# Relative bias read straight from one small table of reversed distances, without per-row copies in DRAM, and the compressed blocks' bias from the same table

## The chip, the cores and the metric

The kernel runs on one core of a Trainium2 chip. The metric is device time in microseconds (us) of one execution; 1440.13 us is the median of 3 runs of the kernel before (1440.06 to 1442.18). The engines are TensorE (PE, matmuls; PEld are its weight loads), VectorE (DVE), ScalarE (ACT), GpSimd (POOL) and SyncE (SP, which here only issues DMAs).

## The reference, cut to what matters

Four layers over 256 tokens of 1024 features: layers 0 and 3 are differential attention, layer 1 is a three-branch sparse attention (compressed blocks, selected blocks, window), layer 2 is attention with a forget gate. Each layer then has a feed-forward part and a gated embedding. Layers 0, 1 and 3 add to every score a bias that depends only on the head and on a bucket of the distance between query and key:

```python
bias = rel_bias[t5_bucket(dist)]            # dist = query position - key position, 32 buckets x 16 heads
s = einsum('bqhcd,bkhcd->bhcqk', qb, k) * scale + bias
pr = masked_softmax(s, dist >= 0)           # layers 0 and 3: 8 pairs of heads, pr[:,:,0] - lam * pr[:,:,1]
...
d_c = t[:, None] - cmp_end[None, :]         # layer 1: distance to the end of block n, cmp_end = 16 n + 31
s_c = einsum('bqgrd,bngd->bgrqn', qc, kc) * scale + rel[t5_bucket(d_c)]
```

## The kernel before

All matmuls of weights run in three passes: an activation on ACT (line 148, `wh`) and a subtraction on DVE (line 149, `wl`) split each 512 KB unit of weights, `raw`, into a high and a low part, and PE multiplies both (lines 170 to 172). `raw` has 5 buffers and is filled by SP; `wh` and `wl` have 8 each. A tile scheduler fixes the order of each engine's instructions when the kernel is built; at run time each engine takes its own list strictly in order. All DMAs of the bias are issued from ACT's list (`QS` is a string of "a" only).

Layer 0 (`diff`) goes like this. `v_proj` projects the values of both token tiles of 128; when tile 0 is done, `between` calls `bias_rows` (line 369): a matmul of a one-hot table of buckets with `rel_bias` gives 16 rows of 512 values, negated bias or a huge number where the key lies ahead of the query, and these go to DRAM as `row`. Then four copies from DRAM to DRAM (line 383) write each head's row 128 times at a pitch of 384 values: `skew`, 4 tiles of 768 KB. `bias_load` (line 409) reads the copies with a step that is one value short of the pitch, so that partition i gets the row shifted by i: `nb`, 128 partitions x 4 heads x 256 keys, two buffers, 12 loads in all, 4 in each of layers 0, 1 and 3. Then `heads` runs the steps of `SEQ`: `K0`, `Q0` and so on split weights, `k0` and `q0` project keys and queries of four heads (`lin_b`, evacuated by ACT at line 436), two digits start an item (four heads of one token tile): scores on PE (line 538), `soft` (line 428 on DVE adds the bias and takes the minimum of the negated scores, line 432 on ACT takes the exponential), transposes (line 506) and products with the values (line 513). The step `b` calls `bias_blocks` (line 395), which loads the one-hot table in the other direction and runs 15 matmuls (line 402) for the 15 compressed blocks, and keeps the result in DRAM as `cmpb`; layer 1 (`nsa`) loads it into the tile `own` (line 755). The output projection follows, then the feed-forward part.

Of the kernel before, what the change touches and what calls it, by code (L numbers as in the profile page):

```python
# [18 lines left out]
P = 128  # L19
# [36 lines left out]
SD = "q0.k0.00.q1.k1.01.10.11.q2.k2.20.21.p.q3.k3.30.p.b.31"  # L56
SEQ = {0: 'K0.Q0.Q1.k0.q0.K1.00.k1.q1.K2.01.Q2.k2.10.q2.20.p.11.21.q3.K3.k3.p.p.p.b.30.31.O.O.O', 2: 'k1.q2.Q0.q1.q0.10.k0.p.11.k3.q3.b.00.01.k2.p.20.p.30.21.p.31', 3: 'K0.Q0.Q1.k0.q0.K1.q1.00.k1.K2.01.Q2.k2.10.q2.20.p.11.21.q3.p.k3.p.p.b.30.31.O.O.O'}
SKEW = 384
# [10 lines left out]
def bucket_table():  # L69
    t = np.zeros((33, 2, 512), np.float32)  # L70
    v = np.arange(512)
    for way, dist in ((0, 255 - v), (1, v - 256)):
        t[rel_bucket(dist), way, v] = -1.0
        t[32, way, v] = (dist < 0).astype(np.float32)
    return t


def shape_consts():
    i = np.arange(P)
    c = np.zeros((P, 2 * P + 1), np.float32)  # L80
    c[:, 0:P] = i[:, None] <= i[None, :]
    c[:, P : 2 * P] = np.where(i[None, :] > i[:, None], BIG, 0.0)
    c[:, 2 * P] = i >= 31
    return c


class Trunk:
# [69 lines left out]
    def unit(self, src, k0, nk, c0, nc):  # L157
        """Rows of chunks k0..k0+nk and columns c0..c0+nc, split: [128, nk, nc]."""
# [3 lines left out]
    def panel(self, src, c0, nc, nk, early=()):  # L162
        """All of 1024 rows in units of nk chunks; [k] gives chunk k's parts [128, nc]."""
# [15 lines left out]
    def later(self, n, key, fn):  # L179
        """Runs fn, which fills a part of key's tiles, after n more products, to issue behind them."""  # L180
# [6 lines left out]
    def flush(self, keys):  # L187
        """Before keys' tiles are read: runs what still has to fill them."""
# [33 lines left out]
    def transpose_split(self, src, hi, lo, t, scale=None, n=KD, c0=0, lag=()):  # L222
        """src [128 tok, n*128] -> hi/lo[:, c0 + c, t*128:(t+1)*128]."""
# [23 lines left out]
    def rms_halves(self, halves):  # L247
        """1 / rms of [half 0, half 1]; each half's square is taken when it is ready."""
# [14 lines left out]
    def prenorm(self, t, g, hT, lag=()):  # L263
        """After the last change of x[t]; takes its halves one after the other."""
# [30 lines left out]
    def startnorm_(self, t, g, hT):  # L295
        """prenorm of the input as it arrives; the second step transposes."""
# [24 lines left out]
    def lin_a(self, src, c0, aT, done, mix, pj=False, cuts=None, early=()):  # L321
        """y[t] = a @ src[:, c0 : c0 + 1024]; token tile 0 runs before tile 1."""
# [12 lines left out]
    def mul_a(self, y, a, w, first, mix):  # L335
        """y += a @ w over a list of chunks. The last ones end the sum, its first half mix chunks ahead of its second."""
# [7 lines left out]
    def lin_b(self, src, c0, hT, w=None):  # L344
        """[256 columns from c0, transposed] = (h @ src)^T in one bank: [128, 2, 256]."""
# [12 lines left out]
    def consts(self):  # L358
# [7 lines left out]
        self.skew = None  # L366
        self.cmp_bias = None

    def bias_rows(self):
        """The bias of every distance, one row per head, then once per query row at a pitch of SKEW."""  # L370
        nc = self.nc
        oh, tab = self.bias_operands(0)
# [4 lines left out]
        row = self.dr.tile([NH, 512], F32, tag="row", name="row")  # L377
        self.dq[QS[0]].dma_start(row, rs)
        self.skew = []
        for u in range(4):  # L380
            sk = self.dr.tile([4, P, SKEW], F32, tag=f"skew{u}", name=f"skew{u}")
            src = bass.AP(tensor=row.tensor, offset=row.offset + 4 * u * 512, ap=[[512, 4], [0, P], [1, SKEW]])
            self.dq[QS[1]].dma_start(sk, src)  # L383
            self.skew.append(sk)

    def bias_operands(self, way):
        nc, a = self.nc, self.a
        oh = self.m2([33, 512])
        nc.sync.dma_start(oh, a["buckets"][:, way, :])
        tab = self.small([33, NH])  # L390
        nc.gpsimd.memset(tab, BIG)
        nc.sync.dma_start(tab[0:32, :], a["rel_bias"])
        return oh, tab
# [762 lines left out]
```

## Time and profile before

| what | value |
|---|---|
| median of 3 runs, lowest, highest | 1440.13, 1440.06, 1442.18 us |
| span of the profiled execution, first to last instruction | 1449.6 us |
| PE busy | 1411.0 us (97% of the span), 8814 instructions |
| DVE, ACT, POOL busy | 855.8, 755.1, 71.9 us |
| mean granted PE clock | 0.979 of full |
| read from HBM, written | 247.61 MB, 4.43 MB |

The span is the profiled execution's own time; no separate time was taken of it, and it is 9.5 us above the median of the runs. PE is busy nearly everywhere, so time can come only from stretches in which PE waits, runs at a lower clock or does work that goes away. Stages are best told apart by stretches of time: layer 0's values end at 37.7 us and its output projection at 168.1 us; the same stage of layer 3 lies at 1139.2 to 1238.7 us.

### The profile page before, as it was taken

The page shows a single profiled execution, that of the slowest core. Times are in us where ns is not written, and L with a number is a line of the kernel's source. Part 1 is how long each engine was busy: PE and PEld are TensorE (multiplying, and loading weights), DVE is VectorE, ACT ScalarE, POOL GpSimd, SP SyncE. Part 2 cuts the span into 40 slices and gives each one's busy share as a digit, 9 for nine tenths or more (in the row PEclk, how much of TensorE's full clock was granted, in tenths as well). Part 3 has the DMA queues.
Part 4 walks back from the last instruction along what each step waited for, and adds up shares of the span by engine and source line. Part 5 has one row for each costly group of instructions (what it writes and reads, how often), then busy time and mean ns, then how long its engine had stood idle before and what let it go on. Part 6 is the DMA issues. An engine that isn't in the chain of part 4 may idle for free.

```text
span 1449.6 us, 22594 instructions
## 1 busy us (share of the span) xinstructions
PE 1411.0 (97%) x8814; PEld 1225.6 (85%) x8814; DVE 855.8 (59%) x1495; ACT 755.1 (52%) x1239; POOL 71.9 (5%) x116
## 2 busy tenths in 40 slices
PE   8589999999999999999999999999999999999998
PEld 6588898998888678998987987998988987999987
DVE  5265765556637656655566555755557577855545
ACT  4255555444625565554446555645446656644443
POOL 1000200000100001000001000000001001100000
PEclk9888999999999899999999999999999999999999
DMA  8564465655575204655645742765646643655642
GB/s 298 177 209 136 136 217 173 202 190 180 164 216 177 77 30 146 225 185 173 202 160 157 257 138 87 233 191 173 203 138 213 221 141 109 213 194 175 203 146 73
DMA packets 155042, 251.41 MB, mean 173 GB/s; under 512 B 10294, under 2 KB 119782, under 8 KB 154936
## 3 DMA queue, kind: packets, MB, share of 16 engines
q1 hardware_dynamic: 144312, 236.44, 50.1%
q10 hardware_dynamic: 10624, 13.53, 3.0%
q8 instruction: 69, 1.13, 0.3%
q14 instruction: 37, 0.30, 0.1%
HBM read 247.61 MB, written 4.43 MB: 174 GB/s over the span
## 4 chain that ended last, share of the span: by engine, by line
PE 68%; issue 21%; DMA 3%; POOL 3%; DVE 2%; ACTq 2%; ACT 2%; DVEq 0%; SPq 0%; POOLq 0%
PE pj L170 11%; PE pj L171 10%; PE pj L172 10%; PE acc L170 9%; PE acc L171 9%; PE acc L172 9%; PE wk L234 2%; PE acc L538 2%; DMA nb<-skew 2%; ACTq L383 2%; PE acc L907 1%; POOL small L213 1%; PE pj L698 1%; PE wk L513 1%; PE wk L658 1%
## 5 line engine op out<-in xcount | busy, mean ns | idle before, releaser
L149 DVE TENSOR_TENSOR wl<-raw,wh 128x1024 fp32r<-128x1024 f32 x421 | 509.9, 1221 | 356.4 <-ACT wh L148 342.6
L148 ACT ACTIVATE wh<-raw 128x1024 fp32r<-128x1024 f32 x421 | 441.9, 1057 | 364.4 <-PE acc L171 149.8
L170 PE MATMUL pj<-big,wh 128*128 128x256 f32 x1248 | 357.2, 286 | 11.8 <-ACT wh L148 11.8
L171 PE MATMUL pj<-big,wl 128*128 128x256 f32 x1248 | 356.2, 285 | 1.1 <-DVE wl L149 1.1
L172 PE MATMUL pj<-big,wh 128*128 128x256 f32 x1248 | 355.5, 285 | 0.0
L170 PEld LDWEIGHTS pj<-big,wh 128*128 128x128 f32 x1248 | 241.1, 193 | 16.2 <-ACT wh L148 12.3
L171 PEld LDWEIGHTS pj<-big,wl 128*128 128x128 f32 x1248 | 241.1, 193 | 5.0 <-DVE wl L149 2.2
L172 PEld LDWEIGHTS pj<-big,wh 128*128 128x128 f32 x1248 | 241.1, 193 | 0.3
L170 PE MATMUL acc<-wh,s 128*128 128x512 f32 x512 | 200.3, 391 | 0.0
L171 PE MATMUL acc<-wh,s 128*128 128x512 f32 x512 | 199.6, 390 | 0.0
L172 PE MATMUL acc<-wl,s 128*128 128x512 f32 x512 | 199.3, 389 | 0.0
L170 PE MATMUL acc<-wh,big 128*128 128x512 f32 (+2 forms) x344 | 132.0, 384 | 0.0
L171 PE MATMUL acc<-wh,big 128*128 128x512 f32 (+2 forms) x344 | 131.1, 381 | 0.0
L172 PE MATMUL acc<-wl,big 128*128 128x512 f32 (+2 forms) x344 | 130.3, 380 | 0.0
L172 PEld LDWEIGHTS acc<-wl,s 128*128 128x128 f32 x512 | 96.1, 188 | 20.3
L170 PEld LDWEIGHTS acc<-wh,s 128*128 128x128 f32 x512 | 96.2, 188 | 18.9
L171 PEld LDWEIGHTS acc<-wh,s 128*128 128x128 f32 x512 | 96.3, 188 | 18.8
L170 PE MATMUL pj<-wh,big 128*128 128x256 f32 (+1 forms) x320 | 100.3, 315 | 0.3 <-ACT big L241 0.2
L171 PE MATMUL pj<-wh,big 128*128 128x256 f32 (+1 forms) x320 | 98.7, 309 | 0.3 <-DVE big L242 0.3
L172 PE MATMUL pj<-wl,big 128*128 128x256 f32 (+1 forms) x320 | 98.3, 307 | 0.0
L432 ACT ACTIVATE s<-s,small 128x128 f32<-128x128 f32 (+1 forms) x160 | 70.7, 446 | 33.8 <-DVE small L428 29.2
L170 PEld LDWEIGHTS acc<-wh,big 128*128 128x128 f32 x344 | 65.6, 191 | 12.6 <-issue 1.0
(209 smaller groups left out, 1545.6 us busy)
## 6 DMA issues: line engine op xcount, KB each, us to landing
raw<-in_mlp_w_dram SPq DMA_DIRECT2D x256, 512.0 KB, 3.9
raw<-in_da_w_in_dram SPq DMA_DIRECT2D x48, 512.0 KB, 5.5
raw<-in_ple_gate_w_dram SPq DMA_DIRECT2D x32, 512.0 KB, 3.5
raw<-in_fox_w_in_dram SPq DMA_DIRECT2D x24, 512.0 KB, 4.1
raw<-in_nsa_w_in_dram SPq DMA_DIRECT2D x18, 512.0 KB, 4.7
g<-in_norm_g_dram SPq DMA_DIRECT2D x16, 512.0 KB, 5.3
raw<-in_da_w_out_dram SPq DMA_DIRECT2D x16, 512.0 KB, 3.3
nb<-skew ACTq DMA_DIRECT2D x12, 512.0 KB, 4.8
```

The lines of the kernel that those rows point to most:

```text
L148: self.nc.scalar.activation(wh, w, AF.Copy),
L149: self.nc.vector.tensor_tensor(wl, w, wh.bitcast(F32), op=ALU.subtract),
L170: mm(out, l[0], r[0], start=first, stop=False)
L171: mm(out, l[1], r[0], start=False, stop=False)
L172: mm(out, l[0], r[1], start=False, stop=last)
L213: nc.gpsimd.tensor_scalar(me, ms, EPS, 1.0, op0=ALU.add, op1=ALU.mult)
L234: z = nc.tensor.transpose(pt[:, c * P : (c + 1) * P], src[:, (b + c) * P : (b + c + 1) * P], self.ident)
L383: self.dq[QS[1]].dma_start(sk, src)
L432: nc.scalar.activation(e[:, b, :], e[:, b, :], AF.Exp, bias=m[:, b : b + 1], scale=-1.0, accum_out=s[:, b : b + 1])
L513: nc.tensor.matmul(po[:, hh * P : (hh + 1) * P], at[:, hh, kb, :], vs[kb][:, h * P : (h + 1) * P], start=kb == 0, stop=kb == nk - 1,)
L538: self.nc.tensor.matmul(sc[c][:, hh * w : (hh + 1) * w], q[cs, hh, qs], k[cs, hh, :w], start=True, stop=True)
L658: nc.tensor.matmul(po[c * HD : (c + 1) * HD, hh * P : (hh + 1) * P], vs[kb][:, h * HD : (h + 1) * HD], at[:, hh, kb, :], start=kb == 0, st ...
```

## The change

`row` is now kept with the distances the other way round, so that a shift by one key and a shift by one query have the same sign in memory, and `bias_load` reads partition i's 256 values directly from `row`, one value further along for each partition. The four copies `skew` are gone. The values arrive in reverse order of the keys; `backwards` makes an access pattern with a step of -1, with which line 428's instruction reads the bias. The table of buckets has one direction. The bias of the compressed blocks is no longer computed by 15 matmuls in layer 0: in layer 1 `bias_blocks` loads shifted pieces of `row` (120 partitions, one for each of 8 heads x 15 blocks, 128 values, two loads), transposes them on PE (two transposes) and DVE copies them, again with a step of -1, into `own`. The step `b` is gone. The rest of the diff takes out comments, which shifts line numbers.

```diff
 def bucket_table():
-    t = np.zeros((33, 2, 512), np.float32)
+    t = np.zeros((33, 512), np.float32)
     v = np.arange(512)
-    for way, dist in ((0, 255 - v), (1, v - 256)):
-        t[rel_bucket(dist), way, v] = -1.0
-        t[32, way, v] = (dist < 0).astype(np.float32)
+    t[rel_bucket(v - 256), v] = -1.0
+    t[32, v] = (v < 256).astype(np.float32)
     return t
...
+def backwards(v):
+    *rest, (step, n) = [list(z) for z in v.ap]
+    return bass.AP(tensor=v.tensor, offset=v.offset + step * (n - 1), ap=[*rest, [-step, n]])
...
     def bias_rows(self):
...
         nc.vector.tensor_copy(rs, pr[:NH, :])
-        row = self.dr.tile([NH, 512], F32, tag="row", name="row")
-        self.dq[QS[0]].dma_start(row, rs)
-        self.skew = []
-        for u in range(4):
-            sk = self.dr.tile([4, P, SKEW], F32, tag=f"skew{u}", name=f"skew{u}")
-            src = bass.AP(tensor=row.tensor, offset=row.offset + 4 * u * 512, ap=[[512, 4], [0, P], [1, SKEW]])
-            self.dq[QS[1]].dma_start(sk, src)
-            self.skew.append(sk)
+        self.row = self.dr.tile([NH, 512], F32, tag="row", name="row")
+        self.dq[QS[0]].dma_start(self.row, rs)
...
-    def bias_blocks(self):
+    def bias_blocks(self, cb):
         nc = self.nc
-        oh, tab = self.bias_operands(1)
+        rows = self.mid([120, 2, P])
         pb = self.wk()
-        for n in range(NCMP):
-            u0 = P - 16 * n - 31 + 256
-            nc.tensor.matmul(pb[:, n * NH : (n + 1) * NH], oh[:, u0 : u0 + P], tab, start=True, stop=True)
-        cb = self.m2([P, NH, NSHIFT])
+        for z in range(2):
+            src = bass.AP(tensor=self.row.tensor, offset=self.row.offset + 129 + 8 * z * 512, ap=[[512, 8], [16, NCMP], [1, P]])
+            self.dq[QS[2]].dma_start(rows[:, z, :], src)
+            nc.tensor.transpose(pb[:, z * 120 : (z + 1) * 120], rows[:, z, :], self.ident[:120, :120])
         nc.gpsimd.memset(cb, BIG)
-        nc.vector.tensor_copy(cb[:, :, 0:NCMP], pb[:, : NCMP * NH].rearrange("p (n h) -> p h n", h=NH))
-        self.cmp_bias = self.dr.tile([P, NH * NSHIFT], F32, tag="cmpb", name="cmpb")
-        self.dq[QS[2]].dma_start(self.cmp_bias, cb.rearrange("p h n -> p (h n)"))
+        pv = pb[:, : NH * NCMP].rearrange("p (h n) -> p h n", n=NCMP)
+        nc.vector.tensor_copy(cb[:, :, 0:NCMP], backwards(pv))

     def bias_load(self, h0):
         nb = self.t([P, 4, S], "nb", 2)
-        k = self.skew[h0 // 4]
-        src = bass.AP(
-            tensor=k.tensor, offset=k.offset + 127,
-            ap=[[SKEW - 1, P], [P * SKEW, 4], [1, S]],
-        )
+        src = bass.AP(tensor=self.row.tensor, offset=self.row.offset + 512 * h0 + 129, ap=[[1, P], [512, 4], [1, S]])
         self.dq[QS[3]].dma_start(nb, src)
...
-                ss.append(self.soft(es[:, c], ..., lambda b: nb[:, 2 * b + c, j0:]))
+                ss.append(self.soft(es[:, c], ..., lambda b: backwards(nb[:, 2 * b + c, :w])))
...
         own = self.s4([P, D])
         ncb = own[:, 0 : NH * NSHIFT].rearrange("p (h n) -> p h n", h=NH)
-        self.dq[QS[8]].dma_start(own[:, 0 : NH * NSHIFT], self.cmp_bias)
+        self.bias_blocks(ncb)
```

ACT's list in layer 0, from the write of `row` on. Before (`s_59` holds the values of token tile 1, `wh_339` and `wh_345` the weights of `K0`, `wh_351` and `wh_357` those of `Q0`):

```order
L378 DMA row<-m_56_256 16x512
L148 ACTIVATE wh_339<-raw_337 128x1024
L148 ACTIVATE wh_345<-raw_343 128x1024
L383 DMA skew_260<-row 512x1x384
L383 DMA skew_262<-row 512x1x384
L383 DMA skew_264<-row 512x1x384
L383 DMA skew_266<-row 512x1x384
L445 ACTIVATE s_59_318<-acc_268 128x512
L445 ACTIVATE s_59_318<-acc_269 128x512
L148 ACTIVATE wh_351<-raw_349 128x1024
L148 ACTIVATE wh_357<-raw_355 128x1024
```

And of the change (line 406 is now `bias_load`, 153 the split, 434 the evacuation of the values; `wh_343` and `wh_349` are now the weights of `Q0`):

```order
L386 DMA row<-m_56_256 16x512
L153 ACTIVATE wh_331<-raw_329 128x1024
L153 ACTIVATE wh_337<-raw_335 128x1024
L406 DMA nb_478<-row 128x4x256
L153 ACTIVATE wh_343<-raw_341 128x1024
L153 ACTIVATE wh_349<-raw_347 128x1024
L153 ACTIVATE wh_355<-raw_353 128x1024
L406 DMA nb_757<-row 128x4x256
L434 ACTIVATE s_59_310<-acc_260 128x512
L153 ACTIVATE wh_361<-raw_359 128x1024
L434 ACTIVATE s_59_310<-acc_261 128x512
```

The four copies have left the list, the first bias load stands in their place, and the splits of `Q0`'s and `Q1`'s weights stand ahead of the evacuations instead of behind them.

PE's list at the end of layer 0's embedding product (`acc` with `m`), ahead of the last items and the output projection. Before:

```order
L172 MATMUL acc_1175<-wl_901,m_189_904 128x512
L402 MATMUL wk_1188<-small_1185,m_254_1183 128x16 x15
L234 MATMUL wk_1211<-ident_65,mid_1209 128x128 x2
L538 MATMUL acc_1248<-s_241_1045 128x128
L538 MATMUL acc_1249<-s_241_1045 128x128
```

And of the change (239 are the transposes of line 234 before, 494 those of line 506, 526 the scores):

```order
L177 MATMUL acc_1167<-wl_893,m_189_896 128x512
L239 MATMUL wk_1177<-ident_65,mid_1175 128x128 x2
L494 MATMUL wk_1188<-ident_65,s_230_1012 128x128 x4
L526 MATMUL acc_1214<-s_241_1037 128x128
L526 MATMUL acc_1215<-s_241_1037 128x128
```

The 15 narrow matmuls are gone, and small matmuls of the items follow the embedding product at once.

PE's list at the start of layer 1, where the normalised input of token tile 1 is transposed (`wk_3541`, `wk_3613`) amid a projection (`pj`). Before:

```order
L170 MATMUL pj_3668<-wh_3591,big_3325 128x512
L234 MATMUL wk_3541<-ident_65,s_691_3530 128x128 x4
L234 MATMUL wk_3613<-ident_65,s_691_3530 128x128 x4
L171 MATMUL pj_3668<-wh_3591,big_3326 128x512
L172 MATMUL pj_3668<-wl_3592,big_3325 128x512
```

And of the change:

```order
L175 MATMUL pj_3641<-wh_3564,big_3291 128x512
L239 MATMUL wk_3507<-ident_65,s_687_3496 128x128 x4
L397 MATMUL wk_3516<-ident_65,mid_3515 128x120 x2
L176 MATMUL pj_3641<-wh_3564,big_3292 128x512
L177 MATMUL pj_3641<-wl_3565,big_3291 128x512
L175 MATMUL pj_3641<-wh_3564,big_3291 128x512
L239 MATMUL wk_3586<-ident_65,s_687_3496 128x128 x4
```

The two transposes of the compressed blocks' bias stand between the two groups of four and take one of the two `wk` banks, so the second group comes three matmuls later, when the first group's bank is free again.

## Rows read from the trace of the kernel before

**Rows 1.** The page: the span, and PE's line of part 1.

```profile
span 1449.6 us, 22594 instructions
...
PE 1411.0 (97%) x8814; PEld 1225.6 (85%) x8814; DVE 855.8 (59%) x1495; ACT 755.1 (52%) x1239; POOL 71.9 (5%) x116
```

**Rows 2.** Stretches: length; PE, PEld, DVE, ACT, POOL busy (instructions); PE clock, DMA share, GB/s.

```profile
43.77:55.61 11.84, 0.00 (x1) 0.00 (x1) 0.02 (x1) 2.08 (x4) 0.00 (x0) 0.66 0.27 101
55.61:61.29 5.68, 5.00 (x22) 4.71 (x22) 5.68 (x5) 4.21 (x5) 0.00 (x0) 0.50 0.69 228
61.29:79.52 18.23, 16.04 (x132) 15.33 (x131) 4.92 (x13) 6.79 (x12) 0.00 (x0) 1.00 0.73 250
79.52:83.28 3.76, 0.02 (x1) 0.00 (x0) 3.73 (x8) 2.90 (x7) 0.00 (x0) 0.80 0.75 203
83.28:92.00 8.72, 8.62 (x34) 6.72 (x35) 7.15 (x23) 4.87 (x12) 0.90 (x2) 0.50 1.00 344
133.91:143.30 9.39, 9.39 (x36) 6.86 (x36) 4.28 (x10) 2.11 (x3) 0.01 (x1) 0.51 0.69 212
37.74:168.10 130.36, 111.05 (x692) 95.70 (x690) 70.26 (x196) 63.02 (x135) 10.25 (x22) 0.87 0.49 160
1139.24:1238.71 99.47, 96.90 (x670) 84.14 (x668) 69.64 (x198) 60.81 (x134) 11.30 (x20) 1.00 0.50 159
```

**Rows 3.** Waits of PE between 40 and 165 us: total, times, longest.

```profile
PE pj L170 <- ACT wh L148: 11.8, 1, 11.8
PE wk L506 <- DVE s L501: 3.7, 1, 3.7
PE acc L538 <- ACT s L436: 1.7, 1, 1.7
```

**Rows 4.** ACT in order of time: start, us, instruction, idle before and its releaser.

```profile
27.64 0.34 ACTq L378 DMA_DIRECT2D row<-m  x1
...
31.51 21.97 ACTq L383 DMA_DIRECT2D skew<-row  x4
53.53 0.60 ACT L445 ACTIVATE s<-acc 128x512 f32<-128x512 f32 x1 [22.75 <-DMA skew<-row]
```

**Rows 5.** The chain that ended last: the first bias load.

```profile
53.98 22.98 DMA nb<-skew
```

**Rows 6.** PE in order of time: the matmuls of the block bias.

```profile
130.03 3.95 PE L402 MATMUL wk<-small,m 33*128 33x16 f32 x30
```

**Rows 7.** PE in order of time at the start of layer 1.

```profile
385.77 1.06 PE L234 MATMUL wk<-ident,s 128*128 128x128 f32 x8 [0.54 <-DVE s L280]
```

**Rows 8.** POOL in order of time there.

```profile
372.23 0.31 POOL L740 MEMSET s<- 128x256 f32 x1
...
384.53 0.55 POOL L214 TENSOR_TENSOR small<-small,nhalf 128x1 f32<-128x1 f32 x1
```

**Rows 9.** DVE in order of time there.

```profile
387.06 1.29 DVE L242 TENSOR_TENSOR big<-wk,big 128x512 fp32r<-128x512 f32 x2 [0.93 <-ACT big L241]
```

**Rows 10.** Line 428 and a bias load in layer 1, in order of time.

```profile
487.93 0.29 DVE L428 CUSTOM_DVE_ANT_0 s<-acc,nb 128x128 f32<-128x128 f32 x1 [3.02 <-PE wk L926]
...
492.71 0.42 DVE L428 CUSTOM_DVE_ANT_0 s<-acc,nb 128x256 f32<-128x256 f32 x1 [2.65 <-PE wk L926]
...
495.05 0.37 ACTq L417 DMA_DIRECT2D nb<-skew  x1
...
498.80 0.43 DVE L428 CUSTOM_DVE_ANT_0 s<-acc,nb 128x256 f32<-128x256 f32 x1 [0.23 <-DMA nb<-skew]
```

**Rows 11.** DMA issues: how many, KB each, median us to landing.

```profile
nb<-skew ACTq DMA_DIRECT2D x12, 512.0 KB, 4.8
...
skew<-row ACTq DMA_DIRECT2D x4, 768.0 KB
nb<-crow ACTq DMA_DIRECT2D x4, 512.0 KB, 4.9
```

**Rows 12.** All instructions of line 428: duration ns, first and last start, forms.

```profile
L428 DVE CUSTOM_DVE_ANT_0 s<-acc,nb x144: 259/416/426, 77.1 to 1218.5; 128x256 f32<-128x256 f32 x80, 128x128 f32<-128x128 f32 x64
```

More of the change, by code (lines that the diff above doesn't have):

```diff
@@ L55 @@
 NSPLIT = 8
-SD = "q0.k0.00.q1.k1.01.10.11.q2.k2.20.21.p.q3.k3.30.p.b.31"
-SEQ = {0: 'K0.Q0.Q1.k0.q0.K1.00.k1.q1.K2.01.Q2.k2.10.q2.20.p.11.21.q3.K3.k3.p.p.p.b.30.31.O.O.O', 2: 'k1.q2.Q0.q1.q0.10.k0.p.11.k3.q3.b.00.01.k2.p.20.p.30.21.p.31', 3: 'K0.Q0.Q1.k0.q0.K1.q1.00.k1.K2.01.Q2.k2.10.q2.20.p.11.21.q3.p.k3.p.p.b.30.31.O.O.O'}
-SKEW = 384
+SD = "q0.k0.00.q1.k1.01.10.11.q2.k2.20.21.p.q3.k3.30.p.31"
+SEQ = {0: 'K0.Q0.Q1.k0.q0.K1.00.k1.q1.K2.01.Q2.k2.10.q2.20.p.11.21.q3.K3.k3.p.p.p.30.31.O.O.O', 2: 'k1.q2.Q0.q1.q0.10.k0.p.11.k3.q3.00.01.k2.p.20.p.30.21.p.31', 3: 'K0.Q0.Q1.k0.q0.K1.q1.00.k1.K2.01.Q2.k2.10.q2.20.p.11.21.q3.p.k3.p.p.30.31.O.O.O'}
 def rel_bucket(dist):
@@ L365, in consts @@
         nc.gpsimd.memset(self.zero, 0.0)
-        self.skew = None
-        self.cmp_bias = None
+        self.row = None
     def bias_rows(self):
-        nc = self.nc
-        oh, tab = self.bias_operands(0)
+        nc, a = self.nc, self.a
+        oh = self.m2([33, 512])
+        nc.sync.dma_start(oh, a["buckets"])
+        tab = self.small([33, NH])
+        nc.gpsimd.memset(tab, BIG)
+        nc.sync.dma_start(tab[0:32, :], a["rel_bias"])
         pr = self.wk()
@@ L376, in bias_rows @@
         nc.vector.tensor_copy(rs, pr[:NH, :])
-        row = self.dr.tile([NH, 512], F32, tag="row", name="row")
-        self.dq[QS[0]].dma_start(row, rs)
-        self.skew = []
-        for u in range(4):
-            sk = self.dr.tile([4, P, SKEW], F32, tag=f"skew{u}", name=f"skew{u}")
-            src = bass.AP(tensor=row.tensor, offset=row.offset + 4 * u * 512, ap=[[512, 4], [0, P], [1, SKEW]])
-            self.dq[QS[1]].dma_start(sk, src)
-            self.skew.append(sk)
[L386 to L393, printed above, removed]
@@ L460, in between @@
                 self.late = None
-            if self.skew is None:
+            if self.row is None:
                 self.bias_rows()
@@ L487, in item @@
             w = nk * P
-            j0 = (1 - t) * P
             sc = self.scores(q, k, slice(t * P, (t + 1) * P), w)
@@ L491, in item @@
             for c in range(2):
-                ss.append(self.soft(es[:, c], lambda b: sc[c][:, b * w : (b + 1) * w], 2, lambda b: nb[:, 2 * b + c, j0:]))
+                ss.append(self.soft(es[:, c], lambda b: sc[c][:, b * w : (b + 1) * w], 2, lambda b: backwards(nb[:, 2 * b + c, :w])))
             for _ in range(DP[i]): yield
@@ L571, in items @@
                     next(self.ple)
-                elif z == "b":
-                    if self.cmp_bias is None:
-                        self.bias_blocks()
                 else:
@@ L748, in nsa @@
         C0 = NH * HD
-        if self.skew is None:
+        if self.row is None:
             self.bias_rows()
-        if self.cmp_bias is None:
-            self.bias_blocks()
         own = self.s4([P, D])
         ncb = own[:, 0 : NH * NSHIFT].rearrange("p (h n) -> p h n", h=NH)
-        self.dq[QS[8]].dma_start(own[:, 0 : NH * NSHIFT], self.cmp_bias)
+        self.bias_blocks(ncb)
         kcT = own[:, 480:608]
@@ L897, in item @@
             w = nk * P
-            j0 = (1 - t) * P
             qs = slice(t * P, (t + 1) * P)
@@ L908, in item @@
                 zs = slice(2 * rr, 2 * rr + 2)
-                self.soft(es[:, rr], lambda b: sc[rr][:, b * w : (b + 1) * w], 2, lambda b: nb[:, r, j0:], m[:, zs], s[:, zs])
+                self.soft(es[:, rr], lambda b: sc[rr][:, b * w : (b + 1) * w], 2, lambda b: backwards(nb[:, r, :w]), m[:, zs], s[:, zs])
             for _ in range(DP[i]): yield
```

## The prediction

> **What bounds the kernel now.** The page comes first: PE is busy 1411.0 of 1449.6 us [rows 1], and a busy share of 97% says that only PE's own gaps, its clock and its work matter. So I went through PE in stretches of 10 us and looked for those that are not full or not at full clock. Nearly all of layer 0's lie in one stage, from the end of its values (37.74 us) to the end of its output projection (168.10 us). Rows 2 cut that stage where PE's state changes: an idle hole of 11.84 us, 5.68 us at half clock (granted 0.50, the level of 1.2 GHz), 18.23 us of which 16.04 are busy, another hole of 3.76 us, 8.72 us at half clock, and late in the stage 9.39 us at 0.51. The last two lines of [rows 2] compare whole stages: layer 0 takes 130.36 us, and the same stage of layer 3, with the same projections and nearly the same steps but with the bias copies long in DRAM, takes 99.47 us, at clock 1.00 throughout. The reader is to see that layer 0 loses over 30 us that are not work.
>
> Next, what PE waits for. The list of waits names ACT's split of weights for the long hole and DVE for the second one [rows 3]. ACT's own order of time says why the split was late: after the write of `row` at 27.64 us ACT issues the four copies, and these issues hold its list from 31.51 us for 21.97 us; the evacuation behind them had waited 22.75 us [rows 4]. DMA engines are busy 0.27 of the time in that hole at 101 GB/s, so they are not full [rows 2]. Then the first bias load follows on the copies and lands 22.98 us after 53.98 [rows 5]; DVE, in order, sits at line 428 until it is there, works off its list afterwards, and that is the second hole.
>
> **Layer 0: what goes.** The copies leave ACT's list, and the first load from `row` stands there. It still waits for the write of `row`, as the first copy did (31.51 us). From then on the splits of `Q0` stand directly behind it, while PE still has the values and `k0` to do until 43.77 us. So:
> - The hole of 11.84 us goes [rows 2].
> - Of the 5.68 us behind it, 0.68 are idle and 5.00 busy at half clock, which at full clock need 2.5: 3.2 us go.
> - In the next 18.23 us, 2.2 are idle; the largest piece, 1.7, is PE waiting for ACT's evacuation of the keys and queries [rows 3], late for the same reason: 2.2 us go.
> - The second hole, 3.7 us, goes with the late load.
> - The 8.72 us behind it at half clock shrink to half: 4.4 us go, as PE did not stand still before them.
> - The 15 matmuls of line 402, which the profile counts as 30, take PE 3.9 us from 130.03 to 133.91 [rows 6]. They go.
> - Behind these narrow matmuls the clock is 0.51 for 9.39 us [rows 2]; at full clock this work needs 4.8: 4.6 us go.
>
> The sum is 11.8 + 3.2 + 2.2 + 3.7 + 4.4 + 3.9 + 4.6 = 33.8 us. As a check, layer 3's stage is 30.9 us shorter although about 2 us of transposes and a wait of its next norm lie in it, so some 33 us by that way.
>
> **Layer 0: what is given back.** Layer 3 shows that the same steps can run with almost no gap, but there the weights are further ahead. I allow 1.5 us of new gaps; the bounds are 0 and 6, the latter the idle us that remain in the stage's later holes (2.2 + 3.7) if only the first one is filled. For the clock in the run of small matmuls ahead of the output projection I allow 1.0 us, between 0 and the 4.6 above, since without line 402 these matmuls still stand in one run. The two early bias loads cost ACT some 0.37 us each, if they issue as line 417 does in layer 1 [rows 10]; ACT's waiting covers that, and without cover it is 0.7.
>
> **The loads from one table.** All partitions now read 4 rows of 2 KB, overlapping. No row shows that, but two come near: the copies read the same rows, and layer 2's load `nb<-crow` gives one 4 KB row to 128 partitions and lands in 4.9 us, while the loads from `skew` take 4.8 [rows 11]. I take no change. In layer 0 the first load has from 31.5 us to about 49.7 to land (`q0`, as long as `k0` with 5.9 us, comes after 43.77), so even 13 us more would be covered. The place without cover is layer 1: a load issued at 495.05 us was awaited until 498.80, that is 3.75 us, and DVE had idled 0.23 [rows 10]. At the copies' 101 GB/s [rows 2] a load of 512 KB takes 5.2 us, 1.4 more than there; two such loads give the upper bound, +2.9 us.
>
> The copies' share of 0.27 is about four of the 16 DMA engines [rows 2]. The Trainium skill (DMA: Bandwidth & Descriptors, section on why a DMA increments its semaphore by 16) says that a DMA runs on the largest number of engines up to 16 that divides the slowest dimension of both sides; the copies have 4 there and the new loads 128, so by it the new loads use all 16 and the +2.9 us is 0. The trace agrees for the copies, and no run here yet shows the new loads.
>
> **Reading backwards.** Line 428 runs 144 times, 80 on 256 and 64 on 128 keys [rows 12], at 0.42 and 0.29 us [rows 10]: 0.13 us for 128 values, about one value per ns and partition. Whether a step of -1 costs more is in no row. Below, it costs nothing; above, a second pass over the values, 0.13 us for every 128, which is 28.7 us of DVE over the kernel. Of these, layer 1's 64 reads (half of each length) are 12.3 us, the only ones in a stage where PE follows DVE closely. I take 0, since the rate is already that of single values.
>
> The Trainium skill (Vector Engine (DVE) Microarchitecture Reference, section 5.1) ties the faster modes of two-source instructions to 2-byte types, so 4-byte values have no mode to lose; it also says that the streaming of a negative step was not measured. That speaks for 0, without settling it.
>
> **The start of layer 1.** The new work stands in the norm of token tile 1. POOL sets `own` to the huge number in an idle spell at 372 us; but a memset like that of 0.31 us now stands ahead of the power at 384.53 [rows 8], on which DVE's scaling and PE's transposes at 385.77 wait, with 0.54 us idle already [rows 7]: +0.3. The two transposes on 120 columns cost about what two of the eight in [rows 7] do, 1.06 / 8 each: +0.25. The second group of four then needs the first group's bank, which DVE leaves after half of its 1.29 us from 387.06 [rows 9], some 0.5 us after PE gets there: +0.5. Together +1.0; bounds 0, if the projection's matmuls fill the gap, and 2.5, if each of the three doubles. The two small loads of the blocks are issued in layer 0's end, long before, and the load of `cmpb` goes.
>
> **Sum.** -33.8 + 1.5 + 1.0 + 1.0 = -30.3 us, on the profiled execution's span of 1449.6, so 1419.3. That execution is 9.5 us over the median of the runs shown; no term hangs on what makes that difference, so I carry -30.3 to the median: 1440.1 - 30.3 = 1410 us.
>
> **Rivals.**
> - Weights set layer 0's pace. For: in layer 0 nothing has been loaded ahead, and the weights of `K1` are issued only once the first splits free their buffers. Against: the DMA engines had room (0.27 in the hole), and layer 3 uses the same 5 buffers. Then the first hole goes, but the later gaps and the half clock behind them stay (2.2 + 3.7 + 4.4 = 10.3): a gain of 20, 1420 us.
> - Backward reads cost a second pass, and layer 1 shows it: +12.3, 1422 us. For: no row shows such a read. Against: the rate above.
> - Slower than before: the one table is a hot spot, and each load takes long. The place is layer 1's pair of loads without cover; each us beyond 3.75 costs one us, twice. To eat up 30.3 us a load must take 3.75 + 15.1 = 19 us; at 20 us the time is 1442. For: 512 pieces out of 8 KB; the first load took 22.98 us. Against: that one had the copies ahead of it, and `crow` lands in 4.9.
> - The change does not free ACT: the loads from `row` hold ACT's list as the copies did, 22 us for four, so 5.5 each. With two of them and three splits ACT comes to about 46 us, and to the weights of `K1` some 3 us after PE could start on them at 49.7: a gap of 3 us and 3 more of half clock behind it, 1416 us. For: the loads stand in the place of the copies, in 512 pieces as well. Against: line 417 issued in 0.37 us [rows 10].
>
> **How the numbers follow.** Main case 0.62, its own range 1405 to 1417 from the bounds (largest gain 33.8; smallest 33.8 - 6 - 2.5 - 2.9 = 22). Weights 0.16, ACT not freed 0.08, backward reads 0.07, hot spot 0.05, which leaves 0.02 for a larger gain. The range 1405 to 1423 leaves out the hot spot, part of the backward case and the larger gain. Two runs of this kernel that differ by under 0.2% (2.9 us) can't be told from no change; every case but the hot spot is faster by more than that: faster 0.95, same 0.01, slower 0.04.
>
> **What would show it.** After: PE busy from 37.7 us on without a hole of over 2 us before the output projection, clock at 1.00 in 50 to 92 us, the stage at 98 to 103 us; ACT's first load from `row` issued at about 31.5 and landed before 45; line 428 at 0.42 and 0.29 us; layer 1's start about 1 us longer. The prediction is wrong if ACT or DVE still hold PE in 44 to 85 us, if loads from `row` take over 8 us, if line 428 lengthens, or if the clock falls in the run of small matmuls as it did behind line 402.

## The result, and the profile after

The changed kernel takes 1411.12 us (median of 4 runs, 1410.44 to 1412.29), the kernel before on the same chip 1441.16 us (4 runs, 1440.06 to 1444.52). The ratio is 0.9774 with a 95% interval of 0.9753 to 0.9795: 30 us faster. The prediction was 1410 with a range of 1405 to 1423, so the size is right. Its reason for the largest part turned out to be half of the story, as the experiments show.

The page of the changed kernel, as in [rows 1]. The profiled execution took 1410.44 us.

```profile
span 1408.6 us, 22528 instructions
...
PE 1386.2 (98%) x8786; PEld 1207.5 (86%) x8786; DVE 855.8 (61%) x1495; ACT 754.5 (54%) x1239; POOL 70.5 (5%) x115
```

DVE's busy time is the same to 0.1 us. PE's fell by 24.8 us, which can't be the removed matmuls alone (3.9 us in [rows 6]). 15.2 us of it lie in layer 0's stage (111.05 us in [rows 2], 95.81 in the last line below), and there the rest is work that ran at half clock before. The other 9.6 lie outside that stage and go by the execution that was profiled: against a second profile of the kernel before, with PE at 1401.5 us, PE's fall is 15.3 us in all.

Stretches of the changed kernel, with the columns of [rows 2]. The last line is layer 0's whole stage, from the end of its values to the end of its output projection.

```profile
36.00:44.00 8.00, 8.00 (x67) 7.88 (x66) 4.81 (x5) 4.71 (x7) 0.00 (x0) 1.00 1.07 336
44.00:52.00 8.00, 8.00 (x70) 7.70 (x69) 5.54 (x15) 5.26 (x13) 0.00 (x0) 1.00 0.92 316
...
100.00:110.00 10.00, 9.70 (x58) 7.74 (x57) 7.43 (x23) 7.17 (x16) 0.57 (x2) 1.00 0.61 185
...
36.40:133.67 97.27, 95.81 (x662) 83.71 (x660) 67.33 (x194) 58.98 (x131) 9.61 (x20) 1.00 0.55 176
```

The reader is to see PE full and at clock 1.00 where the two holes and the half clock stood. The stage went from 130.36 us [rows 2] to 97.27, of which PE is idle for 1.46. The DMA share is worth a second look: while PE runs without a hole, from 36 to 52 us, the DMA engines are full (1.07 and 0.92, above 310 GB/s), where the kernel before had 0.27 in its hole.

PE's waits between 35 and 140 us, as in [rows 3], are all small now; the largest is:

```profile
PE wk L239 <- DVE mid L514: 1.0, 2, 0.8
```

ACT in order of time, against [rows 4]: the write of the row, the two first bias loads, and the first weight split behind the wait for the row.

```profile
26.36 0.33 ACTq L386 DMA_DIRECT2D row<-m  x1
...
31.68 0.39 ACTq L406 DMA_DIRECT2D nb<-row  x1
32.19 1.06 ACT L153 ACTIVATE wh<-raw 128x1024 fp32r<-128x1024 f32 x1 [2.71 <-DMA row<-m]
32.51 0.37 ACTq L406 DMA_DIRECT2D nb<-row  x1
...
130.50 1.04 ACT L211 ACTIVATE m<-x 128x1024 bf16<-128x1024 f32 x1
```

A load from the small table is issued in 0.39 and 0.37 us, and ACT waits 2.71 us in place of 22.75. The last line is a mark that I use for all kernels below: the start of ACT's square in the first norm behind layer 0's mixer (line 206 before the change). **Mark A** stands at 130.50 us here.

The bias loads, and line 417 (428 before), against [rows 11, 12].

```profile
L406 ACTq DMA_DIRECT2D nb<-row x12: 366/367/460, 31.7 to 1152.4; - x12
...
DMA to landing us min/median/max: 3.4/3.9/7.5
```

```profile
L417 DVE CUSTOM_DVE_ANT_0 s<-acc,nb x144: 259/417/426, 49.7 to 1177.4; 128x256 f32<-128x256 f32 x80, 128x128 f32<-128x128 f32 x64
```

The backward reads take 259, 417 and 426 ns where the forward reads took 259, 416 and 426. The loads land in 3.9 us at the median, where those from the copies took 4.8.

### The profile page after: what moved, and what is told of

The parts are those of the page before. It is cut to its first block, busy times and chain, and to the rows that moved or that the text cites. A ratio compares the mean times of both kernels' runs of the same rounds, so it can differ in the third digit from the quotient of the medians.

```text
span 1408.6 us, 22528 instructions
## 1 busy us (share of the span) xinstructions
PE 1386.2 (98%) x8786; PEld 1207.5 (86%) x8786; DVE 855.8 (61%) x1495; ACT 754.5 (54%) x1239; POOL 70.5 (5%) x115
## 4 chain that ended last, share of the span: by engine, by line
PE 48%; issue 21%; POOL 2%; ACT 1%; DMA 1%; DVE 1%; ACTq 0%; DVEq 0%; POOLq 0%
PE pj L175 8%; PE pj L176 8%; PE pj L177 8%; PE acc L175 6%; PE acc L176 6%; PE acc L177 6%; PE acc L889 1%; PE wk L239 1%; PE acc L526 1%; PE wk L643 1%; DMA raw<-in_nsa_w_in_dram 1%; POOL small L218 1%; POOL small L219 1%; PE pj L683 1%; PE wk L637 0%
## 5 line engine op out<-in xcount | busy, mean ns | idle before, releaser
L175 PEld LDWEIGHTS acc<-wh,big 128*128 128x128 f32 x344 | 65.0, 189 | 12.3 <-issue 1.0
```

What stands on the lines that cost most here:

```text
L175: mm(out, l[0], r[0], start=first, stop=False)
```

## Experiments

Medians are compared on one chip where a sentence says so; times in layer 0 are mark A against the changed kernel's 130.50 us in its first profile. Since mark A is taken from one execution each, differences of about 1 us there mean nothing: the changed kernel's three profiles have it at 130.50, 131.49 and 131.60, and the two of the kernel before differ by 2.8.

**The kernel before, once more.** The profile of before that stands ahead of the prediction was of a long execution (span 1449.6 us).

> The kernel before, unchanged, profiled a second time. The spans of the two profiles differ by 41.0 us (1449.6 and 1408.6), the timed runs by 30.0. If the first profile of before was an unusually long execution, this one has a span of 1438 to 1443 us, and the stage of layer 0 (130.4 us then) or the stretches in layers 1 and 2 where the two profiles drift apart by 3.5 and 2.6 us are shorter. If profiles of this kernel are always that much longer, the span is again about 1449 us and nothing moves.

It took 1441.53 us with a span of 1439.7 (PE busy 1401.5), and mark A lies at 162.13 us (164.93 in the first profile). Against this execution layer 0 gains 31.6 us, and the whole span 31.1. The rest of the first profile's extra length lies behind layer 0, and the last section comes back to a part of it.

**The copies without a reader.** The four copies are put back into the changed kernel, and nothing reads them; once from ACT (`"a"`), where they stood, and once from POOL (`"g"`):

```
         self.dq[QS[0]].dma_start(self.row, rs)
+        for u in range(4):
+            sk = self.dr.tile([4, P, 384], F32, tag=f"skew{u}", name=f"skew{u}")
+            src = bass.AP(tensor=self.row.tensor, offset=self.row.offset + 4 * u * 512, ap=[[512, 4], [0, P], [1, 384]])
+            self.dq["a"].dma_start(sk, src)
```

> The changed kernel plus the four copies of 768 KB, issued from ACT where they stood before, and read by nobody. Theory (ACT's list was held): ACT is held some 22 us again, the hole on PE near 44 us comes back with the half clock behind it, and the first bias load, behind the copies on ACT's queue, is late again: 25 us above the changed kernel, about 1436. Rival (traffic): the same time, so this run alone does not tell the two apart. Rival (only the read of the copies mattered, since the loads waited for them): no more than 3 us above the changed kernel, 1414.

> The changed kernel plus the same four unread copies, issued from POOL, so that the traffic stays and ACT's list is free. Theory (ACT's list was held): within 3 us of the changed kernel, 1411 to 1414, no hole on PE in 40 to 60 us. Rival (the 3 MB of copies took DMA time from the weights): as with the copies on ACT, some 20 us above, about 1431, with ACT waiting for raw loads.

From ACT: 1438.06 us (1436.49 to 1441.28), ratio to the kernel before 0.9960 (0.9945 to 0.9974). ACT in order of time shows the old picture, with mark A 24.6 us later:

```profile
32.26 20.53 ACTq L390 DMA_DIRECT2D skew<-row  x4
52.83 0.60 ACT L438 ACTIVATE s<-acc 128x512 f32<-128x512 f32 x1 [22.23 <-DMA skew<-row]
...
155.07 1.04 ACT L211 ACTIVATE m<-x 128x1024 bf16<-128x1024 f32 x1
```

From POOL: 1443.4 us (1437.61 to 1445.9), ratio 0.9985 (0.9968 to 1.0003), no better than before the change. Here ACT's list is free, and yet mark A is 27.9 us late:

```profile
31.50 0.39 ACTq L410 DMA_DIRECT2D nb<-row  x1
...
33.79 0.37 ACTq L410 DMA_DIRECT2D nb<-row  x1
...
52.84 1.06 ACT L153 ACTIVATE wh<-raw 128x1024 fp32r<-128x1024 f32 x1 [9.13 <-DMA raw<-in_da_w_in_dram]
...
158.40 1.06 ACT L211 ACTIVATE m<-x 128x1024 bf16<-128x1024 f32 x1 [0.26 <-issue]
```

So the theory that only ACT's held list costs falls. The bias loads are issued early, at 31.50 and 33.79 us, but the splits now wait for the weights themselves. The DMA view of 30 to 60 us says how late these are (how many, KB each, median us to landing):

```profile
raw<-in_da_w_in_dram SPq DMA_DIRECT2D x8, 512.0 KB, 17.7
```

In the changed kernel the same loads land in 6.3 us in that stretch:

```profile
raw<-in_da_w_in_dram SPq DMA_DIRECT2D x10, 512.0 KB, 6.3
```

The stretches of PE's hole in this kernel (columns as in [rows 2]) show DMA engines that are full, not at the 0.27 of the kernel before:

```profile
44.00:52.00 8.00, 5.51 (x46) 5.30 (x45) 0.97 (x1) 0.00 (x0) 0.00 (x0) 1.00 1.06 330
52.00:60.00 8.00, 1.99 (x8) 1.69 (x10) 4.52 (x4) 5.55 (x7) 0.00 (x0) 0.66 0.92 289
```

Not all of the 27.9 us is the copies' doing. In this kernel the scheduler put the instructions of layer 0 into another order. Behind one split of weights ACT goes on with the exponentials of an item in the changed kernel:

```profile
61.41 1.06 ACT L153 ACTIVATE wh<-raw 128x1024 fp32r<-128x1024 f32 x1
64.81 0.51 ACT L421 ACTIVATE s<-s,small 128x256 f32<-128x256 f32 x1 [2.34 <-DVE small L417]
```

With the copies from POOL four more splits stand ahead of these exponentials:

```profile
74.44 1.06 ACT L153 ACTIVATE wh<-raw 128x1024 fp32r<-128x1024 f32 x1
80.54 1.06 ACT L153 ACTIVATE wh<-raw 128x1024 fp32r<-128x1024 f32 x1 [5.04 <-issue]
...
91.21 0.51 ACT L425 ACTIVATE s<-s,small 128x256 f32<-128x256 f32 x1 [0.66 <-DVE small L421]
```

Up to that split the run is 13.0 us late (74.44 - 61.41). The other 15 come behind it, where PE's, ACT's and DVE's lists differ from the changed kernel's; what the copies alone would have cost there, this run does not show. The other runs keep the order of the kernel that they were made from but for a few entries.

**The same copies, led by 128 rows.** Two things could make the copies so harmful: their bytes, or that they are laid out with the 4 heads outermost and, issued from ACT, keep about four DMA engines busy (0.27 of 16 in [rows 2]). In one kernel the copies of before, still issued from ACT and still read, get the 128 rows outermost; in the other the unread copies from POOL do:

```
-            sk = self.dr.tile([4, P, SKEW], F32, tag=f"skew{u}", name=f"skew{u}")
-            src = bass.AP(tensor=row.tensor, offset=row.offset + 4 * u * 512, ap=[[512, 4], [0, P], [1, SKEW]])
+            sk = self.dr.tile([P, 4, SKEW], F32, tag=f"skew{u}", name=f"skew{u}")
+            src = bass.AP(tensor=row.tensor, offset=row.offset + 4 * u * 512, ap=[[0, P], [512, 4], [1, SKEW]])
...
-            ap=[[SKEW - 1, P], [P * SKEW, 4], [1, S]],
+            ap=[[4 * SKEW - 1, P], [SKEW, 4], [1, S]],
```

> The kernel before, with its four copies of 768 KB still issued from ACT, but the copied tile laid out [128 rows, 4 heads, 384] and its access patterns led by the 128 rows instead of the 4 heads; the bias loads read the new layout. Same bytes, same engine, same place in the program, same 15 matmuls for the blocks. Theory A (a transfer led by 4 runs on few of the 16 DMA engines: in 44:52 us of the kernel before the DMA share was 0.27, four engines' worth, at 100 GB/s): spread, the four copies are issued in under 8 us instead of 21 to 22, ACT's list goes on before 42 us, both holes of layer 0 go but for a few us, and what is left against the changed kernel is the old block bias (7.6 us in the run that put it back) and at most 5 us of the copies' traffic: 1419 to 1425, ratio 0.983 to 0.988. Theory B (the bytes of the copies, or that they are issued from ACT at all, are what costs): 1438 to 1443, ratio 0.997 or more.

> The changed kernel and the same four unread copies from POOL as in the run that cost all of the gain, but led by the 128 rows instead of the 4 heads. Theory A (few DMA engines): the weight loads of 36 to 60 us land in about 6 us again, not 17.7, and the time is 1411 to 1417. Theory B (3.1 MB more to read and to write at the time when the weights come): the same delay as with the narrow copies, 1436 to 1443.

The kernel before with its copies led by 128 rows takes 1422.56 us (1421.32 to 1423.38), ratio to the kernel before 0.9853 (0.9825 to 0.9880). Turning the order of two axes thus gives some 22 of the 29 us that the changed kernel gains on the same chip (1444.33 against 1415.17). ACT in order of time:

```profile
32.22 3.20 ACTq L383 DMA_DIRECT2D skew<-row  x4
35.46 0.60 ACT L445 ACTIVATE s<-acc 128x512 f32<-128x512 f32 x1 [5.96 <-PE acc L172]
```

Four issues take 3.20 us instead of 21.97, and what ended ACT's wait is PE, not a copy. Of the two holes one wait of 4.4 us is left. Theory A's numbers are met: with the same bytes from the same engine, the order of the axes decides how long the list is held.

The unread copies from POOL, led by 128 rows, give 1425.0 us (1423.96 to 1428.57), ratio 0.9875 (0.9845 to 0.9905): 9.8 us over the changed kernel on that chip. Both theories missed: A said at most 6 us, B 25 or more. The DMA view of 30 to 60 us in this kernel:

```profile
DMA packets 5945, 9.17 MB, mean 306 GB/s; under 512 B 266, under 2 KB 4933, under 8 KB 5944
...
q0 software_dynamic: 768, 3.15, 30.6%
...
raw<-in_da_w_in_dram SPq DMA_DIRECT2D x8, 512.0 KB, 14.8
```

The copies' own queue (q0) moves 3.15 MB. At the 306 GB/s of the stretch these are 10.3 us, and mark A, at 141.75 us, is 10.3 us later than in the changed kernel's profile from the same chip (131.49). That the bytes cost just what they take on full engines is an argument from these two equal numbers and not shown further; PE loses the time as a hole, with half clock behind it:

```profile
44.00:52.00 8.00, 4.41 (x37) 4.20 (x36) 0.00 (x0) 0.65 (x1) 0.00 (x0) 1.00 1.00 307
52.00:60.00 8.00, 3.15 (x15) 2.63 (x16) 5.15 (x7) 5.43 (x7) 0.00 (x0) 0.50 0.96 323
```

This run is the clean one of the two from POOL: up to mark A PE, ACT, DVE and SP have the changed kernel's instructions in the changed kernel's order. PE is idle for 8.4 us in these 16, and for 8.5 with the copies led by 4 heads. At the split that stands at 61.41 us in the changed kernel the one is 11.2 us late (72.62), the other 13.0. So from POOL the order of the axes makes some 2 us up to there, and the 17.6 us between the two at mark A are mostly the other order of the lists.

From ACT the same wide copies cost less: mark A of that kernel is at 144.84, or 13.3 us late, of which the old block bias is 7.6 (below), so some 5.7 us. Why less than from POOL was not tried.

**ACT held, no copies.** To price the hold by itself, ACT gets small copies that nothing reads, released by a 32 KB load of the row, and the DMA engines are left alone:

```
+        hold = [self.s4([P, 512]), self.m2([P, 512])]
+        back = self.m2([NH, 512])
+        self.dq["g"].dma_start(back, self.row)
+        with self.tc.high_priority(400):
+            for u in range(44):
+                nc.scalar.activation(hold[u % 2][:NH, :], back, AF.Copy)
```

> The changed kernel, no copies; behind row's write and two or three weight splits ACT is kept busy for some 22 to 24 us by 44 copies of a [16, 512] table that nothing reads (a 32 KB load of the row from DRAM by POOL releases them, as the landing of the row released the four copies before). So ACT is held as before and the DMA engines are left alone; the second bias load is queued behind the hold, the first is not. Theory A (the hold alone costs the first hole: 11.8 idle, 3.2 of half clock, 2.2 behind it): 1425 to 1431. Theory C (the hold cost little, the traffic did it): 1411 to 1416. If the hole comes back but is longer than 11.8 us, the weights that wait for ACT also hold SP's list.

It took 1435.35 us (10 runs, 1432.79 to 1439.36), ratio 0.9944 (0.9924 to 0.9964), more than theory A's 1431. The hold began 6 us later than the copies' and ended at 60.7 us, 7 us later than theirs; PE's hole was 18.5 us. So a run with 30 copies in place of 44 followed:

> The changed kernel with ACT held by 30 instead of 44 copies that nothing reads, so that the hold ends where the four copies' hold ended in the kernel before (about 53.5 us; the run with 44 held it to 60.7 us, with a hole of 18.5 us and 20 us more than the changed kernel). Theory A, that in the kernel before ACT's hold alone would have made the first hole: a hole of 11 to 12 us at 44 us, no second hole (the first bias load stands ahead of the hold), and 12 to 15 us more than the changed kernel on the same chip, ratio to the kernel before 0.986 to 0.991. If the hole is shorter than 10 us, something other than ACT's list set its end.

1429.55 us (1425.99 to 1431.24), ratio 0.9897 (0.9870 to 0.9924), 15.0 us over the changed kernel on the same chip (1414.51). ACT in order of time:

```profile
38.22 0.63 ACT L392 ACTIVATE s<-m 16x512 f32<-16x512 f32 x1 [4.63 <-DMA m<-row]
...
53.83 1.05 ACT L440 ACTIVATE s<-acc 128x512 f32<-128x512 f32 x2
...
146.45 1.04 ACT L211 ACTIVATE m<-x 128x1024 bf16<-128x1024 f32 x1
```

PE's waits in that kernel, between 28 and 140 us:

```profile
PE pj L175 <- ACT wh L153: 11.3, 1, 11.3
```

With the hold ended at 53.8 us as before, the first hole is back at 11.3 us (11.8 in [rows 3]). The second one, by DVE, is not there, since the first bias load stands ahead of the hold. The hold alone thus makes the first hole. That the late bias load made the second follows from its absence here and from the chain in [rows 5]; no run delayed that load alone.

**The block bias of before.** The changed kernel with the 15 matmuls, their step `b` in layer 0, and the detour by DRAM, but with the loads from the one table:

```
-SD = "q0.k0.00.q1.k1.01.10.11.q2.k2.20.21.p.q3.k3.30.p.31"
+SD = "q0.k0.00.q1.k1.01.10.11.q2.k2.20.21.p.q3.k3.30.p.b.31"
...
+        for n in range(NCMP):
+            u0 = P - 16 * n - 31 + 256
+            nc.tensor.matmul(pb[:, n * NH : (n + 1) * NH], oh[:, u0 : u0 + P], tab, start=True, stop=True)
```

> The changed kernel with the old way for the compressed blocks alone: 15 matmuls in layer 0, the result kept in DRAM and loaded in layer 1. Theory (the narrow matmuls cost 3.9 us and drop the clock behind them, and the new way costs 1.0 at the start of layer 1): 3.9 + 4.6 - 1.0 = 7.5 us above the changed kernel, about 1418.6, with a stretch of clock 0.5 behind line 402's matmuls. Rival (the clock fell because of the holes before, not because of these matmuls): only the 3.9 less 1.0, about 1414, clock 1.00. Rival (they were hidden): 1411.

1421.27 us (1416.49 to 1425.06), ratio 0.9833 (0.9800 to 0.9867). PE in order of time, the matmuls and the small ones behind them:

```profile
104.76 3.52 PE L404 MATMUL wk<-small,m 33*128 33x16 f32 x30
...
111.14 2.07 PE L535 MATMUL acc<-s 64*128 64x256 f32 x6
```

The clock behind them, in stretches (1.00 in the 4 us before these):

```profile
108.00:112.00 4.00, 4.00 (x23) 2.74 (x23) 3.16 (x4) 2.13 (x3) 0.00 (x0) 0.64 0.66 203
112.00:116.00 4.00, 4.00 (x15) 3.06 (x14) 0.32 (x1) 0.00 (x0) 0.00 (x0) 0.50 0.88 256
```

Mark A is at 138.12, 7.6 us late: 3.5 of matmuls and some 4 of half clock. Copies (24.6) and blocks (7.6) add up to 32.2, against the 31.6 that layer 0 gained.

**The changed kernel again,** on two chips, beside kernels above.

> The changed kernel again, as it is. 1409 to 1414, ratio 0.976 to 0.980. For the clock of layer 1: that layer took 168 us in the profile of the changed kernel and in the second one of the kernel before, 172 to 174 in the others; if that goes by the execution and not by the kernel, the runs of this one spread over 4 to 6 us with a lower mean clock in the longer ones.

> The changed kernel as it is, beside the two others on the same chip: 1410 to 1416, ratio 0.975 to 0.982; in layer 1 a dip of the clock or none, with 1 to 6 us between the shortest and the longest run.

1415.17 us (1412.76 to 1416.53), ratio 0.9800 (0.9772 to 0.9829), and 1414.51 us (1410.61 to 1417.75), ratio 0.9796 (0.9770 to 0.9822). The kernel before spread more there than at first (1437.68 to 1450.41 and 1439.43 to 1448.89). The gain is 29 us there, with intervals that overlap that of the first result.

**Wider scores in layer 1.** The expectation stands here, the reason for it in the last section.

```
-                    nc.tensor.matmul(sc[:, r * NCMP : (r + 1) * NCMP], qt[hs, r, qs], kcT[hs, 32 * g : 32 * g + NCMP], start=True, stop=True)
+                    nc.tensor.matmul(sc[:, r * P : (r + 1) * P], qt[hs, r, qs], kcT[hs, :], start=True, stop=True)
```

> The changed kernel with one more edit, in layer 1: the scores against the compressed blocks are taken for all four groups (128 columns) instead of the 15 columns that are used, and DVE reads the 15. In profiles of several kernels the granted clock in layer 1 fell behind these matmuls in some executions (0.50 for some 10 us in one, 0.76 and 0.90 for 5 us each in the second profile of the changed kernel) and not in others (1.00 in its first profile), and the layer took 167 to 174 us. Theory N (narrow matmuls bring the clock down): layer 1 is at 1.00 in this profile, 167 to 170 us, and the runs lie at 1408 to 1413, 1 to 4 us under the changed kernel on the same chip. Theory M (the clock falls by something else, or 128 columns cost as much as they give): no difference over 1 us, and dips as before.

1411.88 us (1410.6 to 1412.77), ratio 0.9776 (0.9752 to 0.9801), where the changed kernel had 1414.51 (1410.61 to 1417.75) on the same chip. The median is 2.6 us lower and the spread 2.2 us instead of 7.1, with a granted clock of 0.997 to 0.998 in its five runs and 0.992 to 0.998 in the others, but the intervals of the two ratios overlap: likely a gain, not shown.

## Why the prediction was right, and where its reason was not

**The copies.** Its sum had 11.8 + 3.2 + 2.2 = 17.2 us for the first hole and what follows it, and 3.7 + 4.4 = 8.1 for the second, 25.3 in all. Putting the copies back cost 24.6. The hold alone cost 14.9 us at mark A against the changed kernel on the same chip (146.45 - 131.60), so the first part is some 2 us smaller than put, and the second, which I have only by difference (9.7), some 2 larger. Held against the first profile, as the 24.6 are, the parts are 16.0 and 8.6, so single profiles hardly tell these errors from nothing.

**The reason given for them** was that the four issues hold ACT's list, while the DMA engines, at 0.27, "are not full". The held list is enough for the first hole, as the run without copies shows. But as an argument against the rival in which the weights set the pace the low share failed: the copies from POOL led by 128 rows left ACT free and the lists in the changed kernel's order, and cost 10.3 us, with the weights landing after 14.8 us on full engines.

The hole before had so little traffic for another reason: while ACT holds its list, no buffer of the weights comes free and no load is issued. SP's queue in the kernel before, between 30 and 60 us, waits for the split's second half on DVE (total, times, longest):

```profile
SPq L141 <- DVE wl L149: 32.5, 5, 24.3
```

And in the kernel that holds ACT without copies (30 of the small ones), the stretch in the hole has a DMA share of 0.00:

```profile
44.00:52.00 8.00, 0.60 (x5) 0.39 (x4) 0.00 (x0) 8.00 (x17) 0.00 (x0) 0.84 0.00 0
```

Once loads are issued again behind the copies, a part of them is late. The trace of before has 16 landing events for the weight load issued at 60.24 us: twelve between 64.52 and 65.55 us, the last four between 73.71 and 74.28. That these four wait on the engines that the copies keep busy is my reading; no view shows single engines.

Had the change only moved the copies to POOL, the same reasoning would have promised 25 us, and the run that did it found none (1443.4 us against 1443.79 for the kernel before on that chip), in part by the other order of the lists. The reasoning came out right here because the change removes the hold and the transfer together.

The Trainium skill (DMA: Bandwidth & Descriptors, section on issuing engines not being separate DMA queues) says that DMAs from different engines end on the same 16 DMA engines and interleave there. The runs with copies from POOL agree (17.7 and 14.8 us to landing for weights, 6.3 without them). The same section of the Trainium skill says that issuing from several engines only saves issue time, which is usually small relative to the DMA; here it was 20.53 us for four issues led by 4 heads, and 3.20 us led by 128 rows, so for the first layout the measurement decides otherwise. The Trainium skill's rule for authors on that page (Use all 16 engines), to put a dimension of a multiple of 16 outermost, is borne out by 1422.56 us against 1444.33.

**The blocks** were put at 3.9 + 4.6 = 8.5 us, and measured 7.6.

**What is given back.** New gaps of 1.5 us: PE is idle for 1.46 us of the stage. 1.0 us of half clock in the run of small matmuls ahead of the output projection: not there, the clock stayed at 1.00 in 100 to 110 us, in all three profiles of the changed kernel. So these matmuls did not lose the clock where the narrow ones of line 402 were not in front.

**The loads and the backward reads** were both put at 0, and the traces agree (3.9 us to landing, and 417 against 416 ns). The bounds of 2.9 and 12.3 us were not reached. Layer 3's mixer, which reads the bias as well, takes 113.0 us from the square of token tile 1 in its own norm to the first square in the next, in the first profile of either kernel (1118.72 to 1231.72 us before, 1077.69 to 1190.71 after).

**The start of layer 1** was put at 1.0 us: 0.3 by POOL's memset, 0.25 by two transposes and 0.5 by the bank. Against the second profile of before, DVE's scaling starts 4.28 instead of 4.03 us after ACT's square (350.66 - 346.38 and 382.03 - 378.00), so 0.25 is POOL's. The last transposed half leaves PE's bank 8.28 instead of 7.27 us after it, 1.0 later in all, but PE does not wait for that: the projection's matmuls fill the time, which was the prediction's lower bound. PE comes to its next product 8.61 instead of 8.13 us after the square (354.99 - 346.38 and 386.13 - 378.00). So the term was 0.5 us on PE, POOL's part and the transposes, and the bank's was nothing. POOL in the changed kernel, in order of time, where the memset of 0.31 us now stands ahead of the power, as against [rows 8]:

```profile
349.80 0.31 POOL L725 MEMSET s<- 128x256 f32 x1
350.07 0.55 POOL L219 TENSOR_TENSOR small<-small,nhalf 128x1 f32<-128x1 f32 x1
```

DVE's scaling there, and PE's transposes behind it, which waited for it 0.78 us, against 0.54 in [rows 7]:

```profile
350.66 0.90 DVE L285 TENSOR_SCALAR s<-s,small 128x512 f32<-128x512 f32 x2 [0.97 <-POOL small L219]
...
351.31 0.63 PE L239 MATMUL wk<-ident,s 128*128 128x128 f32 x4 [0.78 <-DVE s L285]
```

PE's next product in the changed kernel, and in the second profile of before:

```profile
354.99 0.28 PE L175 MATMUL acc<-wh,big 128*128 128x256 f32 x1
...
386.13 0.28 PE L170 MATMUL acc<-wh,big 128*128 128x256 f32 x1
```

**The sum** was -30.3 us. The spans differ by 31.1 against the second profile of before, the medians by 30.0. That it came so near is in part luck. The prediction says that no term hangs on what made its profile long, but 2.8 us of that lie in layer 0: layer 0 gains 31.6 us against the second profile and 34.4 against the first, from which the terms were read, where the prediction had 33.8 - 2.5 = 31.3. And errors offset each other: the gain by copies and blocks was put 1.6 us too high, but what the clock would take back 1.0 too high and layer 1's start 0.5. Layer 0's stage took 97.27 us, just under the 98 to 103 that were to show it. The prediction's smallest gain of 22 also leaves out the 4.6 us that it allows for the clock.

## What to carry to other kernels

A low DMA share does not say that there is room: ask whether a held list kept other loads from being issued, and how many engines the transfer occupies. A transfer led by a short axis can cost by holding the list of the engine that issues it, by delaying loads of other queues, and by what is queued behind it; moving it to POOL took away the hold only. Before a copy is designed away, turn its axes: here that alone gave some three quarters of the gain. And before two runs are compared, see that their lists have the same order: an edit of one transfer can make the scheduler arrange a whole layer anew, and the difference is then not the transfer's alone.

## What the hardware showed that was not expected

Layer 1's mixer, measured from the square of token tile 1 in its own norm to the first square in the next, took 167.0 to 174.3 us over thirteen profiles, and not by kernel: 168.2, 169.8 and 173.1 us in the three of the changed kernel, 171.8 and 167.4 in the two of the kernel before. The difference is in the clock. PE in order of time in the changed kernel's third profile, from the second of two such groups of matmuls on:

```profile
445.30 2.77 PE L846 MATMUL wk<-s,s 64*128 64x15 f32 x16
...
448.52 2.07 PE L889 MATMUL acc<-s,s 64*128 64x256 f32 x4
```

And the same instructions in its first profile:

```profile
443.03 1.53 PE L846 MATMUL wk<-s,s 64*128 64x15 f32 x16
...
444.81 1.13 PE L889 MATMUL acc<-s,s 64*128 64x256 f32 x4
```

In the third profile, the stretch around it (columns as in [rows 2]):

```profile
442.00:452.00 10.00, 10.00 (x43) 7.39 (x42) 4.64 (x15) 3.02 (x9) 0.00 (x0) 0.56 0.39 119
```

The same instructions in the same order run at half clock (0.56 in the mean of the stretch) in one execution and at 1.00 in another, behind groups of matmuls with 15 columns each. The matmuls of line 402, with 16 columns, show the same pattern in [rows 2, 6] and in the run that put them back. In the kernel with 128 columns in their place the two groups take 1.71 us each, 0.18 more than those of 15 columns at full clock, and the stretch keeps its clock:

```profile
442.00:452.00 10.00, 10.00 (x62) 6.79 (x61) 6.54 (x37) 4.47 (x15) 0.00 (x0) 1.00 0.34 110
```

Its layer 1 took 167.4 us in that execution, though a dip (0.89 in 512 to 522 us) came later there. One profile and five runs don't settle whether narrow matmuls are the cause or one of several. What they do settle is how to read such a kernel: a difference of 4 to 6 us between two single profiles can be this dip and nothing else.
